# Spectra kept in DRAM as real and imaginary rows side by side, stored and loaded by one transfer per four frequencies

## The chip, the cores and the metric

The kernel runs on one core of a Trainium2 chip. The metric is the device time of one execution in microseconds (us). The kernel before took 2328.96 us (median of 3 runs, 2328.45 to 2333.43).

## What is computed

One layer of an encoder block on 2048 positions of 1024 channels, all in float32. The input is normalised and projected; one quarter of the projection goes through a two-dimensional Fourier transform, the rest through a Hyena operator; both are normalised and projected back, and an MLP follows.

```python
h   = RMSNorm(x)
p   = h @ W_in            # [Fourier group | Hyena x1 | x2 | v], 512 columns each
y_f = RMSNorm_f(Re(FFT2 over positions and group channels))
y_h = RMSNorm_h(Hyena: z = v; for n, gate in (x1, x2): z = gate * long_conv(z, k[n]))
x   = x + concat(y_f, y_h) @ W_out
x   = x + relu(RMSNorm(x) @ W_fc1)^2 @ W_fc2
out = RMSNorm_final(x)

def fft_long_conv(u, k_freq, d):        # the long convolution, twice per channel
    uf = rfft(u, n=2 * l)
    y = irfft(uf * k_freq, n=2 * l)[:, :l]
    return y + u * d
```

The change touches `k_freq`, the spectra of the long filters: 512 channels, two orders, 2048 frequencies, complex.

## The kernel before, in words

The work goes in stages on TensorE (PE): the projections (`project`), the Fourier group (`fourier`), the filters and their spectra (`filters`), the two long convolutions (`hyena`), then the output projection and the two MLP layers, which take most of the time. Transforms are matrix products in two steps, 64 x 64, with a transpose by VectorE (DVE) between.

**The filters.** A `Unit` is 128 channels (`ct`, 0 to 3) of one order (`n`, 0 or 1), eight units in all. `generate` makes the filter in eight pieces; every second piece loads 512 KB of a decay table (`dec`, two buffers). `stage1` is the first transform step (`mm3`, then a transpose into `Gk`), `stage2` the second: for each `q` of 0 to 7 four products of 128 x 128 into one PSUM bank (`pk2`, L572), one per frequency slot. On the 128 partitions of that bank stand 64 real rows and then 64 imaginary rows; the free axis is 4 slots x 128 channels. ScalarE (ACT) copies the bank to the SBUF tile `ks` (L575). Two `q` share one tile of 8 slots (three buffers), and after the second SyncE (SP) issues a store of 512 KB to the DRAM tensor `spec` of that unit (L577): 128 rows of 4 KB. That is 4 stores per unit, 32 in all. Stages of one unit and generation of the unit after next are interleaved by hand (`GENERATE`).

**The convolutions.** A `Block` is 128 channels of one order, eight blocks. `first` and `second` are the two transform steps of the signal. For each `q`, `spectrum` (L647) loads the spectrum of four slots into a tile `ks` of [128, 2, 4, 128] (four buffers), in which each half of the partitions holds both the real (index 0) and the imaginary part (index 1): the complex product needs the real part beside both halves of `pz2`, and the imaginary part beside both halves of the turned copy `zs`. In DRAM the real rows are the first 64 of `spec` and the imaginary rows the last 64, so L650 views them as 64 partitions x 2 parts x 2 KB, and L651 and L652 send this to the lower and then to the upper half of the partitions: two transfers of 256 KB per `q`, 16 per block, 128 in all. At `q` = 0 two small operations (L655, L657) set the slot of the zero frequency right. Then ACT makes `zs` (L676, L677), DVE multiplies by the real part (L679), GpSimd (POOL) by the imaginary part (L680), one of them adds (L681), and `inverse` (L689) needs the sum `y`. `load` (L645) brings the gate of a block, `xg`, 1 MB in rows of 512 B. The loop at L714 interleaves three blocks: the second step of one, the inverse of the one before, the first step of the next, whose first spectrum is loaded at `q` = 7.

All these transfers are issued by SP, which takes them in program order and waits at each until its buffer is free or its source is written. A scheduler orders each engine's instructions from the order of the code and its own estimates.

Of the kernel before, what the change touches and what calls it, by code (L numbers as in the profile page):

```python
# [10 lines left out]
F32 = mybir.dt.float32  # L11
# [116 lines left out]
P = 128  # L128
# [6 lines left out]
def hybrid_block(ctx: ExitStack, tc: tile.TileContext, A, out):  # L135
    nc = tc.nc
# [4 lines left out]
    def scratch(name, shape):  # L141
        return dram.tile(shape, F32, tag=name, name=name)

    gd = [scratch(f"gates{i}", [P, NT, 512]) for i in range(3)]
    kd = [[scratch(f"spec{i}{n}", [P, 32, 128]) for n in range(2)] for i in range(4)]
    wfd = scratch("wfd", [1024, 512])
    embd = scratch("embd", [P, 32, P])
    xtd = [scratch(f"xt{t}", [P, 8, P]) for t in range(NT)]
# [13 lines left out]
    def pool(name, side="left"):  # L162
        return tc.tile_pool(name=name, bufs=1, side=side, reuse_waits="tile")

    def pa(nm):
        return ps.tile([P, 512], F32, tag="a", name=nm, bufs=8)
# [304 lines left out]
    def filters(ctx, fp, gp, zp, zzs, norms, emb, wo, e1k, f2):  # L471
# [9 lines left out]
        p = pa("plongd")  # L481
# [3 lines left out]
        class Unit:  # L485
# [83 lines left out]
            def stage2(self, q):  # L569
                p = pa("pk2")  # L570
                for j in range(4):
                    nc.tensor.matmul(p[:, 128 * j : 128 * j + 128], lhsT=f2[:, 4 * q + j, :], rhs=self.G[:, :, 4 * q + j], start=True, stop=True)  # L572
                if q % 2 == 0:
                    self.ks = sp.tile([P, 8, 128], F32, tag="ks", name="ks", bufs=3)
                nc.scalar.copy(self.ks[:, 4 * (q % 2) : 4 * (q % 2) + 4, :], p.rearrange("p (f c) -> p f c", f=4))  # L575
                if q % 2:
                    nc.sync.dma_start(kd[self.ct][self.n][:, 4 * q - 4 : 4 * q + 4, :], self.ks)  # L577

        units = [Unit(ct, n) for n in range(2) for ct in range(4)]
        for u in units[:2]:  # L580
# [7 lines left out]
        sp = ctx.enter_context(pool("spectra", "right"))  # L588
# [41 lines left out]
    def hyena(hp, wp, rp, zz, e1, b1, f2, a2, out_weights, out_ahead):  # L630
# [6 lines left out]
        class Block:  # L637
# [9 lines left out]
            def spectrum(self, q):  # L647

                ks = hp.tile([P, 2, 4, 128], F32, tag="ks", name="ks", bufs=4)
                src = kd[self.ct][self.n][:, 4 * q : 4 * q + 4, :].rearrange("(s p) f c -> p s f c", s=2)  # L650
                for hf in (slice(0, 64), slice(64, 128)):  # L651
                    nc.sync.dma_start(ks[hf], src)  # L652
                if q == 0:

                    nc.scalar.copy(ks[64:65, 0, 0, :], ks[64:65, 1, 0, :])  # L655
                    for h in (0, 64):
                        nc.gpsimd.memset(ks[h : h + 1, 1, 0, :], 0.0)  # L657
                return ks
# [742 lines left out]
```

## Time and profile before

| what | value |
|---|---|
| median of 3 runs | 2328.96 us |
| the profiled execution, its own time | 2339.88 us |
| its span, first to last instruction | 2336.8 us |
| busy: PE, weight loads, DVE, ACT, POOL | 96%, 80%, 65%, 47%, 36% |
| mean granted TensorE clock | 0.986 |
| moved by DMA, mean rate | 468.42 MB, 200 GB/s |
| stores of spectra issued | 484.7 to 637.5 us |
| loads of spectra issued | 638.0 to 840.2 us |

The table is from one profiled execution. The span is divided by the views into stretches with the busy time of each engine, the share of time for which the core's 16 DMA engines were busy on average, and the rate at which they moved bytes. A wait names who waited and for whom, with total, count and longest. "Us to landing" is the time from the issue of a transfer to its completion.

### The profile page before, as it was taken

To read this page: it belongs to the slowest core of one execution; us is meant where nothing else is said; L and a number is where in the kernel's file an instruction comes from. 1 tells how busy PE (TensorE), PEld (TensorE's weight loads), DVE (VectorE), ACT (ScalarE), POOL (GpSimd) and SP (SyncE) were. 2 spreads that over 40 slices of the span, in tenths; PEclk is the share of its full clock that TensorE was granted. 3 is DMA by queue.
4 is the path that set the end of the run, shared out by engine and by line. 5 is a ranking of instruction groups with operands and counts; after the bars stand their busy time and mean duration, and the time that the engine had idled before them with its cause. 6 is when DMAs were issued, how large, how long until landed. Compare 5 with 4: busy or idle time off the path is not lost. (4 is left out here: it accounts for less than half of the span.)

```text
span 2336.8 us, 31028 instructions
## 1 busy us (share of the span) xinstructions
PE 2250.9 (96%) x11025; PEld 1860.4 (80%) x11025; DVE 1514.5 (65%) x2248; ACT 1106.6 (47%) x1826; POOL 840.6 (36%) x633
## 2 busy tenths in 40 slices
PE   7999998999899979998999999999999999999998
PEld 6887787799787858886788877888888888888886
DVE  6998666677577774547544457444466666866667
ACT  6554211466455554544555556555543333533334
POOL 3345322567465522215755556555400000000000
PEclk9999999999999989999999999999999999999999
DMA  7535888457688986567544456444479666866631
GB/s 250 181 137 176 290 308 321 144 199 233 214 201 188 200 218 189 177 182 237 161 150 152 152 204 208 152 150 149 149 279 373 234 191 198 284 207 193 198 117 72
DMA packets 294780, 468.42 MB, mean 200 GB/s; under 512 B 18453, under 2 KB 142687, under 8 KB 290273
## 3 DMA queue, kind: packets, MB, share of 16 engines
q1 hardware_dynamic: 291265, 460.43, 61.9%
q10 hardware_dynamic: 3360, 6.02, 0.8%
q8 instruction: 86, 1.41, 0.3%
q14 instruction: 69, 0.57, 0.1%
HBM read 312.54 MB, written 152.27 MB: 199 GB/s over the span
## 5 line engine op out<-in xcount | busy, mean ns | idle before, releaser
L181 ACT CAST qahm<-ra 128x1024 fp32r<-128x1024 f32 x110 | 116.0, 1054 | 345.8 <-PE p2u L190 172.0
L182 DVE TENSOR_TENSOR qalm<-ra,qahm 128x1024 fp32r<-128x1024 f32 x110 | 134.7, 1224 | 154.8 <-ACT qahm L181 151.7
L1183 POOL TENSOR_TENSOR acc<-acc,gfin 128x512 f32<-128x512 f32 x4 | 5.1, 1278 | 632.9 <-DMA out<-acc 625.4
L189 PE MATMUL pu<-wh,xh 128*128 128x512 f32 x512 | 206.4, 404 | 5.8 <-ACT wh L184 4.8
L190 PE MATMUL pu<-wl,xh 128*128 128x512 f32 x512 | 203.3, 397 | 5.9 <-DVE wl L182 3.7
L191 PE MATMUL pu<-wh,xl 128*128 128x512 f32 x512 | 203.2, 397 | 5.7 <-DVE xl L182 5.7
L190 PE MATMUL p2u<-qblm,qahm 128*128 128x512 f32 x504 | 196.2, 389 | 0.3 <-DVE qblm L182 0.3
L189 PE MATMUL p2u<-qbhm,qahm 128*128 128x512 f32 x504 | 195.9, 389 | 0.0
L191 PE MATMUL p2u<-qbhm,qalm 128*128 128x512 f32 x504 | 195.8, 389 | 0.0
L397 POOL TENSOR_TENSOR acc<-acc,cw 128x512 f32<-128x512 f32 x45 | 60.9, 1353 | 206.1 <-DVE acc L374 204.8
L182 DVE TENSOR_TENSOR qblm<-rb,qbhm 128x1024 fp32r<-128x1024 f32 x110 | 134.0, 1219 | 1.1 <-ACT qbhm L181 1.1
L181 ACT CAST ahm<-s 128x512 fp32r<-128x512 f32 x124 | 76.7, 621 | 94.0 <-PE p1v L190 54.1
L190 PEld LDWEIGHTS pu<-wl,xh 128*128 128x128 f32 x512 | 98.3, 192 | 28.7 <-DVE wl L182 4.1
L191 PEld LDWEIGHTS pu<-wh,xl 128*128 128x128 f32 x512 | 98.2, 192 | 28.3 <-DVE xl L182 7.7
L189 PEld LDWEIGHTS pu<-wh,xh 128*128 128x128 f32 x512 | 98.0, 192 | 27.8 <-ACT wh L184 6.2
L182 POOL TENSOR_TENSOR alm<-W,ahm 128x512 fp32r<-128x512 f32 x63 | 85.5, 1358 | 91.4 <-ACT ahm L181 91.4
L181 ACT CAST qbhm<-rb 128x1024 fp32r<-128x1024 f32 x110 | 115.3, 1048 | 4.6 <-DMA a1m<-c 2.8
L190 PEld LDWEIGHTS p2u<-qblm,qahm 128*128 128x128 f32 x504 | 94.6, 188 | 20.3 <-DVE qblm L182 0.8
L189 PEld LDWEIGHTS p2u<-qbhm,qahm 128*128 128x128 f32 x504 | 94.6, 188 | 20.2 <-issue 0.3
L191 PEld LDWEIGHTS p2u<-qbhm,qalm 128*128 128x128 f32 x504 | 94.6, 188 | 19.6
L181 ACT CAST ahm<-W 128x512 fp32r<-128x512 f32 x94 | 57.6, 615 | 103.4 <-PE p1u L190 100.8
L191 PE MATMUL p1u<-bm,alm 128*128 128x512 f32 x252 | 99.9, 396 | 6.4 <-DVE alm L182 6.4
(387 smaller groups left out, 6456.8 us busy)
## 6 DMA issues: line engine op xcount, KB each, us to landing
W<-in_w_fc SPq DMA_DIRECT2D x66, 512.0 KB, 4.6
ks<-spec SPq DMA_DIRECT2D x128, 256.0 KB, 6.8
rb<-td SPq DMA_DIRECT2D x64, 512.0 KB, 4.1
ra<-a1m SPq DMA_DIRECT2D x56, 512.0 KB, 6.0
ra<-a0m SPq DMA_DIRECT2D x54, 512.0 KB, 10.7
rb<-in_w_fc SPq DMA_DIRECT2D x46, 512.0 KB, 4.5
f<-in_w_fc SPq DMA_DIRECT2D x16, 1024.0 KB
td<-f SPq DMA_DIRECT2D x16, 1024.0 KB, 4.7
```

The lines of the kernel that those rows point to most:

```text
L181: nc.scalar.copy(hi, src)
L182: (eng or nc.vector).tensor_sub(lo, src, hi)
L189: nc.tensor.matmul(o, lhsT=lh, rhs=rh, start=start, stop=False, skip_group_check=more)
L190: nc.tensor.matmul(o, lhsT=lh, rhs=rl, start=False, stop=False, skip_group_check=more)
L191: nc.tensor.matmul(o, lhsT=ll, rhs=rh, start=False, stop=stop, skip_group_check=more)
L397: nc.gpsimd.tensor_add(m1, m1, cw[:, 3, :])
L1183: nc.gpsimd.tensor_mul(acc[i][:, c], acc[i][:, c], gfin[:, c])
```

## The change: what it does, and the diff

The DRAM tensor of a unit's spectrum has the shape [64, 8, 2, 512] in place of [128, 32, 128]: for each of 64 rows, for each `q`, the 512 real numbers and then the 512 imaginary ones, 4 KB in one piece.

The store is made for every `q`: 256 KB from a tile of [128, 512], of which six buffers stand in the room of the three larger ones. Its DRAM side is viewed as 2 parts x 64 rows x 2 KB, with a step of 2 KB between the parts and of 32 KB between rows. There are 64 stores in place of 32.

The load is one transfer per `q`: 64 rows of 4 KB, read twice by a leading dimension of 2 with a step of 0, to 128 partitions of 4 KB. There are 64 loads of 512 KB in place of 128 of 256 KB. The bytes that arrive are the same.

```diff
-    kd = [[scratch(f"spec{i}{n}", [P, 32, 128]) for n in range(2)] for i in range(4)]
+
+    kd = [[scratch(f"spec{i}{n}", [64, 8, 2, 512]) for n in range(2)] for i in range(4)]
...
-                if q % 2 == 0:
-                    self.ks = sp.tile([P, 8, 128], F32, tag="ks", name="ks", bufs=3)
-                nc.scalar.copy(self.ks[:, 4 * (q % 2) : 4 * (q % 2) + 4, :], p.rearrange("p (f c) -> p f c", f=4))
-                if q % 2:
-                    nc.sync.dma_start(kd[self.ct][self.n][:, 4 * q - 4 : 4 * q + 4, :], self.ks)
+                ks = sp.tile([P, 512], F32, tag="ks", name="ks", bufs=6)
+                nc.scalar.copy(ks, p)
+                nc.sync.dma_start(kd[self.ct][self.n].rearrange("p q s x -> s p q x")[:, :, q], ks)
...
                 ks = hp.tile([P, 2, 4, 128], F32, tag="ks", name="ks", bufs=4)
-                src = kd[self.ct][self.n][:, 4 * q : 4 * q + 4, :].rearrange("(s p) f c -> p s f c", s=2)
-                for hf in (slice(0, 64), slice(64, 128)):
-                    nc.sync.dma_start(ks[hf], src)
+                src = kd[self.ct][self.n][:, q].rearrange("p s x -> p (s x)")
+                nc.sync.dma_start(ks.rearrange("p s f c -> p (s f c)"), src.unsqueeze(0).broadcast_to([2, 64, 1024]))
```

PE's instructions stand in the same order as before. On SP the order around the two kinds of transfer changes. At the start of the filters' stores, SP's instructions before (a row gives the line, what is written and read, and the counts of the written side, outermost first; `spec_60`, `spec_62` and so on are the tensors of the units, `dec` a table's piece):

```order
L577 DMA spec_60<-ks 128x1024 x2
L170 DMA dec<-in_decay 128x1024
L577 DMA spec_60<-ks 128x1024 x2
L170 DMA dec<-in_decay 128x1024 x3
L577 DMA spec_62<-ks 128x1024 x2
```

Each store has 128 as its outermost count. The same place with the change:

```order
L576 DMA spec_60<-ks 2x64x512 x4
L171 DMA dec<-in_decay 128x1024
L576 DMA spec_60<-ks 2x64x512 x4
L171 DMA dec<-in_decay 128x1024 x3
L576 DMA spec_62<-ks 2x64x512 x4
```

Twice as many stores stand between the same loads, and the outermost count of what a store writes is 2. At the start of the convolutions, SP before (`ks` is the tile of a spectrum, `xg` the gate's):

```order
L652 DMA ks<-spec_60 64x2x512 x14
L652 DMA ks<-spec_62 64x2x512 x2
L652 DMA ks<-spec_60 64x2x512 x2
L652 DMA ks<-spec_62 64x2x512 x6
L645 DMA xg<-gates_58 128x16x128
L652 DMA ks<-spec_62 64x2x512 x6
```

Loads of a spectrum come in pairs, one for each half of the partitions. With the change (`yf` is a tile of the Fourier group's result, needed by the output projection):

```order
L650 DMA ks<-spec_60 128x1x1024 x4
L644 DMA xg<-gates_58 128x16x128
L650 DMA ks<-spec_60 128x1x1024
L644 DMA xg<-gates_58 128x16x128
L650 DMA ks<-spec_60 128x1x1024 x2
L650 DMA ks<-spec_62 128x1x1024
L650 DMA ks<-spec_60 128x1x1024
L774 DMA yf<-yfd 64x2x256
L650 DMA ks<-spec_62 128x1x1024
```

The row shows the written side alone, whose outermost count is 128; the read side's is the 2 of the repeated reading. The loads of the gate and those of the first `yf` tiles have moved ahead, the latter from behind the last spectrum to the first blocks.

## The prediction, as put on record before the run

> **What bounds the kernel now.** I read the page first, then the stretches of the two stages that the change touches, then the transfers in them.
>
> ```profile
> span 2336.8 us, 31028 instructions
> ...
> PE 2250.9 (96%) x11025; PEld 1860.4 (80%) x11025; DVE 1514.5 (65%) x2248; ACT 1106.6 (47%) x1826; POOL 840.6 (36%) x633
> ...
> DMA packets 294780, 468.42 MB, mean 200 GB/s; under 512 B 18453, under 2 KB 142687, under 8 KB 290273
> ```
>
> PE is busy for 96% of the span: it is the bound of the whole, and a transfer matters only where it starves PE. When the spectra are stored and loaded stands in the view of the tensor `spec` (duration of an issue, then first and last start):
>
> ```profile
> L652 SPq DMA_DIRECT2D ks<-spec x128: 573/605/4610, 638.0 to 840.2; - x128
> L577 SPq DMA_DIRECT2D spec<-ks x32: 319/320/1562, 484.7 to 637.5; - x32
> ...
> DMA to landing us min/median/max: 2.9/6.0/9.6
> ```
>
> So the filters' stores fill 484.7 to 638, and the convolutions' loads 638 to 840. Those two stretches by engine, and a third from the second MLP layer in which the DMA engines were never idle (the last two columns are their mean busy share and rate):
>
> ```profile
> core 0: us, PE busy (x) PEld busy (x) DVE busy (x) ACT busy (x) POOL busy (x), PEclk, DMA share, GB/s
> 484.50:638.00 153.50, 143.93 (x1054) 130.67 (x1053) 104.20 (x182) 85.71 (x172) 100.02 (x83) 0.98 0.64 217
> 638.00:840.00 202.00, 190.22 (x1323) 165.32 (x1321) 152.11 (x236) 110.67 (x192) 116.55 (x104) 0.99 0.88 199
> ...
> 1740.00:1780.00 40.00, 40.00 (x178) 32.93 (x177) 28.81 (x32) 18.06 (x18) 0.00 (x0) 1.00 1.05 390
> ```
>
> PE is busy for 143.9 of 153.5 us and 190.2 of 202 us, so 9.6 and 11.8 us are all that faster transfers could win in the two. The DMA engines are busy for 0.64 and 0.88 of the time: in the second stage they have little to spare, even with all sixteen at work. In that stage this is who waits for a spectrum, or for a product that needs one:
>
> ```profile
> POOL zs L680 <- DMA ks<-spec: 27.4, 16, 6.0
> ...
> PE pv L689 <- DVE y L681: 13.2, 12, 3.8
> ```
>
> POOL waits 27.4 us for spectra, and PE's 13.2 us of waiting for `y` are partly what follows from it.
>
> **On how many engines a transfer runs.** The question is how the new shapes are spread. Their outermost counts are 2 on one side (the DRAM side of the store, the repeated side of the load) and 128 on the other. The trace has transfers whose outermost count is 128 or 64, and a few with 63. All of the convolutions' stretch:
>
> ```profile
> GB/s 255 233 152 217 204 193 111 269 232 229 198 129 238 232 138 235 80 118 269 228 224 200 67 266 232 228 232 47 264 213 228 231 83 183 238 234 229 159 168 258
> DMA packets 32197, 40.13 MB, mean 199 GB/s; under 512 B 2075, under 2 KB 16411, under 8 KB 32180
> ...
> ks<-spec SPq DMA_DIRECT2D x127, 256.0 KB, 6.8
> xg<-gates SPq DMA_DIRECT2D x7, 1024.0 KB, 12.7
> ```
>
> No row of these transfers is under 512 B, and yet there are 2075 such packets for 134 transfers: 15.5 each, that is 16 but for the edges of the stretch. I read them as one closing packet from each engine that took part. The queue of ACT, which at 25 to 60 us carries only the neighbours' rows of the projection, tests that reading:
>
> ```profile
> GB/s 407 407 426 398 335 225 183 169 19 148 155 229 386 243 120 211 346 302 311 150 112 183 224 256 151 188 55 0 0 0 37 66 206 435 410 337 7 5 152 215
> ...
> q10 hardware_dynamic: 608, 1.04, 11.1%
> ...
> nb<-full ACTq DMA_DIRECT2D x4, 128.0 KB, 2.3
> nb<-full ACTq DMA_DIRECT2D x4, 126.0 KB
> ```
>
> Four transfers of 64 rows of 2 KB (L384, L387) and four of 63 (L385, L388) leave 608 packets. With 16 closing packets for each of the first, 4 x (64 + 16) = 320 are theirs, and 288 are left for the others: 72 each, 63 rows and 9 closing packets. Nine is the largest number up to 16 that divides 63. So a count that sixteen does not divide costs engines, and for an outermost count of 2 the same reading gives two engines. The Trainium skill says this outright (DMA: Bandwidth & Descriptors, Rules for kernel authors, the row on using all 16 engines): a leading zero-stride broadcast of c copies confines the whole transfer to at most c engines. The trace agrees for 63 rows; no transfer of it has a repeated outermost dimension, so for that case the page stands alone.
>
> **The price of one engine.** When all sixteen are busy (1740 to 1780 us) they move 390 GB/s: 24.4 GB/s each. The highest slice above, 435, gives 27.2; the filters' stretch gives 217 / (16 x 0.64) = 21.2. I take 24.4, the row in which nothing but the engines bounds, and keep 27.2 and 21.2 as the ends. The convolutions' own 199 / (16 x 0.88) = 14.1 comes from small rows and from sixteen engines that write to half the partitions at once, and is left out.
>
> **The stores, part by part.** A store moves 256 KB, 131,072 B on each of two engines: 5.37 us at 24.4 GB/s (4.82 to 6.18). 64 of them are 344 us. The other transfers of that stretch:
>
> ```profile
> spec<-ks SPq DMA_DIRECT2D x32, 512.0 KB, 3.7
> dec<-in_decay SPq DMA_DIRECT2D x20, 512.0 KB, 4.0
> zz<-gates SPq DMA_DIRECT2D x4, 1024.0 KB
> a<-in_a SPq DMA_DIRECT2D x1, 2048.0 KB
> ```
>
> Each engine was busy 0.64 x 153.5 = 98 us there, of which the old stores took 32 x 32,768 B / 24.4 GB/s = 43, so 55 us stay for the rest. The two engines need 344 + 55 = 399 us for what PE gives out in 153.5: they become the bound of the stage, which grows by 245 us. Behind a late store wait, in turn, its buffer (one of six), ACT's copy, PE's next bank. The decay loads run on all engines, and so wait on these two behind up to six stores; where a load then comes late, the two run dry for some us. Twelve such places with up to 4 us each bound that at 0 to 50 us; I take nothing, as two `dec` buffers let SP ask ahead.
>
> The 64 issues on SP cost nothing: at some 0.6 us each (L652's row) they are 38 us in 399. ACT's copies are the same 64.
>
> **The loads.** A load moves 512 KB into SBUF, 262,144 B on each of two engines: 10.74 us (9.64 to 12.36). 64 of them are 688 us. The eight gate loads come on top. In the rates above, each `xg` shows as about one slice of 5 us with a low rate (111, 80, 67, 47, 83), so 8 x 5 = 40 us (30 to 50). Together 728 us; before it was 638.0 to the landing of the last load, 840.2 + 6.8 = 847, or 209 us. The stage grows by 519 us. With four buffers and a `q` that takes PE some 3 us (202 us by 64), the next load is always queued, so the two engines never idle. SP's issues fall from 128 to 64, which is worth nothing, since SP would not be waited for. The `yf` loads that moved ahead are off the path: after 847 the old order had them on it, but I see at most a few us there and count none.
>
> The skill also has a price for one engine, about 27 GiB/s (same page, Specifications). By it a load would take 9.0 us and the time would come to about 2930 us; the measured rate stands against it.
>
> **The sum.** 2339.88 + 245 + 519 = 3104 us for a profiled execution. That of before lies 11 us above the median of the runs, so **3093 us**. With 27.2 GB/s and the small ends (308 + 50 and 617 + 30) it is about 2970; with 21.2 GB/s and some dry time (396 + 55 + 40 and 791 + 50) about 3300.
>
> **The rivals.**
>
> *It does what it is written to do, on sixteen engines.* Then the rows of a load double to 4 KB and the writes go to all partitions at once; the wait for spectra goes and PE's idle 11.8 us of the second stage shrink. The skill's rule on two transfers to disjoint partition halves (same table: they share the engines, use one 128-partition transfer) would have it so. The time would be 2317 at best; half of the idle time is other waits, so 2323. What speaks for it: the SBUF side does count 128, and a generator could split by that. What speaks against: 63 rows got nine engines and were not split otherwise. It decides by the number of engines: 33.55 MB at 24.4 GB/s are 1375 engine-us, and 202 - 40 us are free for them, so from nine engines on the stage stays PE's, and below it the loads set its length. Chance 0.06, most of it faster.
>
> *The transfer is made as two halves after all,* each of 64 rows on sixteen engines, as before: 2329, no change. Chance 0.02.
>
> *Only one kind is confined.* If the store is split by its SBUF side, 2329 + 519 = 2848; if only the store is confined, 2329 + 245 = 2574. Both sides of both kinds carry a 2 and a 128, so I see no reason for a difference: 0.02.
>
> *Two engines are enough,* because alone they run faster. To hide the loads each would have to move 16.8 MB in 162 us, 104 GB/s, four times the best slice: no chance of its own.
>
> **How the numbers follow.** The confined case has 0.90, and nine tenths of it lie in 2970 to 3300; the range is that, 0.81 in all. A change of 0.2% (5 us, the spread of the three runs) is what can be told from none. Faster 0.05, same 0.03, slower 0.92.
>
> **What would show it.** If two engines carry each new transfer, packets under 512 B fall from 18453 by 160 x 16 and rise by 128 x 2, to about 16,150; with sixteen they would be about 17,940. The DMA share of the convolutions falls to about 0.2, the rate to under 60 GB/s, the waits for `ks<-spec` grow to hundreds of us, and a load lands some 40 us after its issue, four deep in the queue. PE's busy time stays near 2250 us. A stage of the convolutions near 200 us with a DMA share under 0.88 would prove the step on the engines wrong; loads spaced by much more or less than 10.7 us would prove the price wrong.

## The result, and the profile after

The changed kernel took 3045.41 us (median of 4 runs, 3040.69 to 3050.72), the kernel before in the same sessions 2330.1 us: a ratio of 1.3068, with a 95% interval of 1.3036 to 1.3099. 3093 us were forecast, in a range of 2970 to 3300. The profiled execution of the changed kernel took 3045.94 us, with a span of 3044.2 us: 707.4 us more than the span before.

The page of the changed kernel, its busy line and the rows of its slices (each 76 us):

```profile
span 3044.2 us, 31007 instructions
...
PE 2372.4 (78%) x11025; PEld 1950.8 (64%) x11025; DVE 1514.4 (50%) x2248; ACT 1105.7 (36%) x1826; POOL 839.5 (28%) x633
...
PE   8998996555533333444349989999999999999998
...
PEclk9999998877666766767669999999999999999999
DMA  7447953233121111111145565446444497676651
GB/s 238 167 157 281 338 190 116 79 102 110 76 66 63 53 63 62 63 62 64 57 143 173 177 225 165 149 145 223 162 150 150 167 386 233 193 238 232 194 186 56
DMA packets 288380, 468.41 MB, mean 154 GB/s; under 512 B 16149, under 2 KB 140383, under 8 KB 283873
```

The same two rows before (each slice 58 us):

```profile
PE   7999998999899979998999999999999999999998
...
DMA  7535888457688986567544456444479666866631
```

The hole is in plain sight: between the 7th and the 21st slice PE is busy for about half of the time and then for a third, and the DMA engines fall with it, in the longer second part to a tenth or two of their time and to some 60 GB/s. PE starves there, and little moves. Before the 7th and behind the 21st slice PE is busy for most of the time, as it was throughout in the kernel before. The bytes are the same but for 0.01 MB (468.41 MB), and the packets under 512 B are 16149, where the text on record had "about 16,150" for two engines per new transfer.

The tensor `spec` in the changed kernel (issue time min/median/max, first and last start; then who waited for it, total us and times):

```profile
L576 SPq DMA_DIRECT2D spec<-ks x64: 485/4788/11188, 478.2 to 849.4; - x64
L650 SPq DMA_DIRECT2D ks<-spec x64: 482/5427/21207, 854.5 to 1534.5; - x64
...
  ACT ks L653: 371.3, 8
  DVE y L677: 322.0, 45
  POOL ks L655: 312.4, 8
  POOL zs L678: 308.0, 39
  ACT ks L575: 77.8, 18
```

ACT, DVE and POOL, which touch a loaded spectrum, now wait for it, for over 300 us each, and the copies of the filters wait for their stores (78 us). The stretches of the two stages and of what follows (the columns are those of the table by engine: busy time, then granted clock, DMA share and GB/s):

```profile
478.20:854.50 376.30, 203.00 (x1142) 173.57 (x1140) 104.92 (x191) 86.56 (x174) 100.55 (x84) 0.76 0.26 89
854.50:1560.50 706.00, 265.76 (x1284) 222.11 (x1284) 156.36 (x243) 117.09 (x205) 120.00 (x107) 0.65 0.19 63
1560.50:3044.00 1483.50, 1450.28 (x6440) 1186.64 (x6440) 882.36 (x1234) 709.16 (x1118) 423.15 (x294) 0.99 0.58 190
```

The filters take 376 us from the first store to the first load (153 before). From there to 1560.5 us, where the last wait for a spectrum ends, it is 706 us (209 before). What follows takes 1483.5 us, against 1490 from 847 us on before.

How wide a single transfer is can be read off a stretch of 20 us in which nothing but loads of spectra moves:

```profile
1000.00:1020.00 20.00, 5.82 (x31) 5.36 (x32) 6.62 (x12) 7.96 (x15) 6.27 (x5) 0.57 0.13 52
```

A share of 0.13 of sixteen engines is two engines, and 52 GB/s are 26 GB/s for each. The packets fit: before, the trace has 18070 packets of 4 B, now 15766. The 2304 fewer are 160 x 16 - 128 x 2, which is one such closing packet for each engine of a transfer.

### The profile page after: what moved, and what is told of

Its sections match the earlier page's. It is cut to its first block, busy times and chain, and to the rows that moved or that the text cites. A ratio compares the mean times of both kernels' runs of the same rounds, so it can differ in the third digit from the quotient of the medians.

```text
span 3044.2 us, 31007 instructions
## 1 busy us (share of the span) xinstructions
PE 2372.4 (78%) x11025; PEld 1950.8 (64%) x11025; DVE 1514.4 (50%) x2248; ACT 1105.7 (36%) x1826; POOL 839.5 (28%) x633
## 2 busy tenths in 40 slices
DMA packets 288380, 468.41 MB, mean 154 GB/s; under 512 B 16149, under 2 KB 140383, under 8 KB 283873
## 5 line engine op out<-in xcount | busy, mean ns | idle before, releaser
L687 PE MATMUL pv<-y,a 128*128 128x128 f32 x512 | 105.2, 371 | 305.1 <-ACT V L688 133.2
L687 PEld LDWEIGHTS pv<-y,a 128*128 128x128 f32 x512 | 92.5, 271 | 318.6 <-ACT V L688 134.6
L677 DVE TENSOR_TENSOR y<-pz,ks 128x512 f32<-128x512 f32 x64 | 43.8, 685 | 377.5 <-DMA ks<-spec 322.0
L671 PE MATMUL pz<-G,f 128*128 128x128 f32 x512 | 95.1, 342 | 107.4 <-DVE G L419 48.8
L678 POOL TENSOR_TENSOR zs<-zs,ks 128x512 f32<-128x512 f32 x64 | 82.7, 1297 | 347.0 <-DMA ks<-spec 308.0
L671 PEld LDWEIGHTS pz<-G,f 128*128 128x128 f32 x512 | 89.9, 254 | 118.7 <-DVE G L419 51.6
L664 PE MATMUL pz<-zz,e1z 128*128 128x256 f32 x256 | 91.8, 506 | 52.7 <-ACT V L688 25.5
L573 PE MATMUL pk<-Gk,f 128*128 128x128 f32 x512 | 76.7, 309 | 64.2 <-DVE Gk L419 59.7
L509 DVE TENSOR_TENSOR kt<-pk,dec 128x512 f32<-128x512 f32 x64 | 43.0, 678 | 153.7 <-DMA dec<-in_decay 146.0
```

The lines of the kernel that those rows point to most:

```text
L509: nc.vector.tensor_mul(k4, p.rearrange("p (l c) -> p l c", l=4), dec)
L664: nc.tensor.matmul(p[:, 256 * sp : 256 * sp + 256], lhsT=e1[:, sp, :], rhs=zz[:, :, lo : lo + 16], start=True, stop=True)
L677: nc.vector.tensor_mul(y, p3, ks[:, 0])
L678: nc.gpsimd.tensor_mul(zs, zs, ks[:, 1])
L687: nc.tensor.matmul(p[:, 128 * j : 128 * j + 128], lhsT=a2[:, 4 * q + j, :], rhs=self.y[q][:, j, :], start=True, stop=True)
```

## The experiments

Theory **T1**: an outermost count of 2 puts a transfer on two DMA engines, and that alone makes the time. Rivals: **T2**, the new layout is slow (row pitch, smaller stores, more of them); **T3**, reading a row twice by a step of 0 is slow; **T4**, any order of rows but one plain run is slow. All edits are made to the changed kernel unless it is said otherwise.

**Neither transfer with a count of 2.**

```diff
-                nc.sync.dma_start(kd[self.ct][self.n].rearrange("p q s x -> s p q x")[:, :, q], ks)
+                for s, hf in enumerate((slice(0, 64), slice(64, 128))):
+                    nc.sync.dma_start(kd[self.ct][self.n][:, q, s], ks[hf])
...
-                nc.sync.dma_start(ks.rearrange("p s f c -> p (s f c)"), src.unsqueeze(0).broadcast_to([2, 64, 1024]))
+                for hf in (slice(0, 64), slice(64, 128)):
+                    nc.sync.dma_start(ks[hf].rearrange("p s f c -> p (s f c)"), src)
```

> The new layout in DRAM is kept; each store is made as two of 64 rows (real, then imaginary), each load as two of 64 rows of 4 KB, one for each half of the partitions. No transfer has an outermost count of 2. Theory T1 (an outermost count of 2 puts a transfer on two DMA engines, and nothing else is slow): back to the time of before, 2310 to 2340 us. Rival T2 (the layout itself is slow: a row pitch of 32 KB, 256 KB stores, six small buffers, more transfers on SP): most of the 715 us stay, over 2800 us.

Measured: 2355.98 us, 1.0088 of before (1.0059 to 1.0118). With the same layout 689 of the 715 us are gone: T2 falls. But it is not the time of before; 21 us are left, outside what T1 expected. They lie in the filters. The stretch from the first store to the first load, and PE's waits in it:

```profile
483.40:666.50 183.10, 159.71 (x1084) 144.05 (x1083) 108.18 (x188) 86.87 (x173) 100.83 (x84) 0.91 0.72 186
```

```profile
PE pdk L545 <- DVE dk L534: 10.8, 4, 3.8
PE psum_k L529 <- POOL acc L523: 8.6, 2, 7.4
```

PE's longest wait there before (it had none for `dk`):

```profile
PE psum_k L528 <- POOL acc L522: 6.2, 1, 6.2
```

The stage takes 183 us where it took 153. PE waits 10.8 us for `dk`, a small product in the normalising of a filter, for which it did not wait before, and its granted clock, the share of its full clock that it is given, is 0.91 in place of 0.98. The loads' stage is 197 us long, 5 less than before. The last runs below come back to the filters.

**One term at a time.** The stores as in the change with the loads in halves, and the reverse.

> Stores as in the change (outermost count 2), loads as two halves of 64 rows. T1: the store's term alone. In the trace of the change the stretch from the first store to the first load is 376 us where it was 153, so 2330 + 223 = 2553 us (2530 to 2590). If stores cost nothing by themselves (only the loads are confined): 2330 us.

> Stores as two halves of 64 rows, loads as in the change (one transfer, a leading count of 2 with step 0). T1: the load's term alone, 680 us from the first load to the last where it was 202: 2330 + 478 = 2808 us (2780 to 2860). If the two terms add up, this and the run with confined stores together make 2330 + 715. T2: no smaller than the change's 3045 us, since the layout is the same.

Measured: 2560.5 and 2841.57 us, one run each, beside 2334.95 for before. The transfers of `spec`, for the confined stores and for the confined loads:

```profile
L651 SPq DMA_DIRECT2D ks<-spec x128: 444/594/4694, 856.6 to 1062.1; - x128
L576 SPq DMA_DIRECT2D spec<-ks x64: 478/4798/11001, 480.3 to 851.4; - x64
```

```profile
L577 SPq DMA_DIRECT2D spec<-ks x128: 445/580/1757, 476.5 to 658.1; - x128
L651 SPq DMA_DIRECT2D ks<-spec x64: 474/5852/21253, 659.5 to 1328.3; - x64
```

Both times lie within what was expected. Each stage is long only where its own transfer has the count of 2: 376 us for the stores, 669 us for the loads. Each page counts 18069 packets under 512 B, which is what two engines for the one kind and sixteen for the other give (18453 - 32 x 16 + 64 x 2 for the stores). The extra times are 226 and 507 us; the second kernel has the half stores, which with half loads cost 21 us, so 226 + 486 = 712 against the change's 715. The terms add up.

**The repetition kept, the count changed.**

```diff
-                nc.sync.dma_start(ks.rearrange("p s f c -> p (s f c)"), src.unsqueeze(0).broadcast_to([2, 64, 1024]))
+                nc.sync.dma_start(ks.rearrange("p s f c -> p (s f c)"), src.unsqueeze(1).broadcast_to([64, 2, 1024]))
```

> Stores as two halves; one load of 512 KB per q that reads each row twice, as in the change, but with the 64 rows as the outermost count and the repetition inside it. The rows then land two by two on neighbouring partitions, so the spectra meet the wrong numbers: only the time counts. T1: 64 is spread over sixteen engines, 2310 to 2335 us, and this is what the change would have given had its transfer been spread. Rival T3 (reading a row twice by a step of 0 is what is slow, whatever its place): 2800 us and more.

Measured: 2339.84 us, 1.0022 of before (1.0010 to 1.0033), 5 us above the top of what T1 expected. The row is still read twice by a step of 0, in one transfer of 512 KB, and 500 us of the load's term are gone: T3 falls. Filters and loads by stretch:

```profile
483.70:667.20 183.50, 159.86 (x1084) 144.34 (x1083) 108.26 (x188) 86.91 (x173) 100.90 (x84) 0.91 0.72 185
667.20:852.80 185.60, 181.30 (x1282) 158.48 (x1281) 144.19 (x235) 111.47 (x195) 116.23 (x104) 0.99 0.74 225
```

The convolutions take 186 us from the first load to the last, 17 less than before, and move 225 GB/s at a DMA share of 0.74 where it was 199 at 0.88. So the merging of two halves does help when it is spread over all engines. The half stores, which this kernel needs too, take it back: the filters are at 183 us again. An engine moved 225 / (16 x 0.74) = 19.0 GB/s while busy, and 199 / (16 x 0.88) = 14.1 with the halves of before, so with the halves each of the sixteen engines was also slower. The length of a row has little to do with it: the kernel with halves has the same rows of 4 KB and moved 203 GB/s at 0.86 in its loads, 14.8 for each engine. The Trainium skill (DMA: Bandwidth & Descriptors, Rules for kernel authors) would have one transfer over all partitions in place of two over halves, since both share the same engines. The trace agrees with the advice, and shows that the shared engines are not the whole reason.

**The count without the repetition: 2, 4 and 8.** Two loads of 64 rows for each `q`, with the rows in k interleaved runs; stores in halves. The edit for a count of 2 (4 and 8 in place of the last number otherwise):

```diff
-                nc.sync.dma_start(ks.rearrange("p s f c -> p (s f c)"), src.unsqueeze(0).broadcast_to([2, 64, 1024]))
+                for hf in (slice(0, 64), slice(64, 128)):
+                    nc.sync.dma_start(ks[hf].rearrange("p s f c -> p (s f c)"), src.rearrange("(a b) x -> b a x", b=2))
```

> As the run with all transfers in halves (2356 us), but each load of 64 rows takes them in another order: row 0, 2, 4 ... and then 1, 3, 5 ..., so that its outermost count is 2 (2 x 32 rows of 4 KB). No row is read twice. The spectra meet the wrong frequencies; only the time counts. T1: two engines again, 128 loads x 131,072 B / 26 GB/s = 645 us and 40 for the gates in place of 197: 2356 + 488 = 2844 us, as with the repeated read (2842); packets under 512 B 18453 - 160 x 16 + 128 x 16 + 128 x 2 = 18197. T3 (the repetition is what is slow): 2356 us.

> The same with the rows taken in four interleaved runs, outermost count 4. T1: four engines, 128 x 65,536 B / 26 GB/s = 323 + 40 = 363 us in place of 197: 2356 + 166 = 2522 us (2490 to 2550); packets under 512 B 18453. Rival T4 (any order other than one run over all rows falls back to a slow path, whatever the count): about 2840 us.

> The same with eight interleaved runs, outermost count 8. T1: eight engines, 161 + 40 = 201 us of transfers against the 197 that the stage takes without them as a bound: 2356 to 2385 us; packets under 512 B 18965. This is the point from which the number of engines decides, put at nine in the prediction with the lower rate. T4: about 2840 us.

Measured: 2837.4, 2524.6 and 2396.42 us, one run each, beside 2335.26 for before. The rates from 700 to 850 us, in the middle of the loads, for counts of 2, 4 and 8 in this order (each number is a slice of 3.75 us):

```profile
GB/s 52 51 51 52 52 52 51 56 52 52 51 51 52 52 52 51 51 52 210 112 47 55 52 42 46 52 52 52 50 52 52 52 51 51 52 52 52 50 57 52
```

```profile
GB/s 107 104 105 105 150 207 101 104 82 99 104 102 105 105 105 102 116 223 127 105 86 94 105 105 105 104 106 93 102 178 187 102 96 67 97 103 108 105 104 104
```

```profile
GB/s 202 167 201 202 209 208 91 173 220 150 152 153 172 196 201 210 226 181 208 206 201 144 82 185 211 192 208 209 206 125 156 226 152 167 196 211 208 114 167 212
```

The plateaus are 52, 104 and 208 GB/s: 26 GB/s for each unit of the count. The packets under 512 B over the whole program were 18197, 18453 and 18965, each the expected number to the last packet. T3 and T4 fall, and T1 holds at five numbers of engines: 2, 4 and 8 by rate and packets, 9 (the 63 rows) and 16 by packets. Eight engines kept 26 GB/s each while they wrote to half the partitions; the 14.8 above are for sixteen at once. The count of 8 came out at 2396 us, above the 2385 expected: its loads fill 232 us, not 201. By the sums the transfers and PE's work are nearly equal there, and POOL's products wait 73 us for `ks` in that stage; that each side holds up the other now and then is how we read it, and no run separates it.

**Can the gain be kept?** Three kernels in which all that is stored and loaded is spread. In the first the spectrum stands twice in DRAM, on 128 rows, and one load of 128 rows brings it.

```diff
-    kd = [[scratch(f"spec{i}{n}", [64, 8, 2, 512]) for n in range(2)] for i in range(4)]
+    kd = [[scratch(f"spec{i}{n}", [P, 8, 2, 512]) for n in range(2)] for i in range(4)]
...
+                if q % 2 == 1:
+                    for d, queue in ((slice(0, 64), nc.sync), (slice(64, 128), nc.scalar)):
+                        for s, hf in enumerate((slice(0, 64), slice(64, 128))):
+                            queue.dma_start(kd[self.ct][self.n][d, q - 1 : q + 1, s], self.ks[hf])
...
-                nc.sync.dma_start(ks.rearrange("p s f c -> p (s f c)"), src.unsqueeze(0).broadcast_to([2, 64, 1024]))
+                nc.sync.dma_start(ks.rearrange("p s f c -> p (s f c)"), src)
```

> A version meant to be right and spread: the spectrum stands twice in DRAM, 128 rows of 32 KB, so that one load of 128 rows of 4 KB fills both halves of the partitions on sixteen engines. For each pair of q there are four stores of 64 rows (real and imaginary part, to each copy), two of them issued by ACT. T1: the convolutions take 186 us where before took 202, as in the run with the repetition inside (16 us won); the stores move twice the bytes, 33.5 MB, some 43 us more of DMA time in a stage with 55 free. 2315 us if the filters stay at 153 us, 2345 if they take 183 as with the half stores. If transfers on two engines were not the cause, it would stay above 2800.

Measured: 2342.99 us, 1.0043 of before (1.0026 to 1.0059): 16 us won in the loads (661.7 to 848.3 us), 26 lost in the filters (482.7 to 661.7). The higher of the two expectations.

The second asks whether the filters lose by the number of stores or by the order of the engines' work. It is the kernel with halves, with stores for two `q` at once:

```diff
...
+                if q % 2:
+                    for s, hf in enumerate((slice(0, 64), slice(64, 128))):
+                        nc.sync.dma_start(kd[self.ct][self.n][:, q - 1 : q + 1, s], self.ks[hf])
...
```

> As the run with all transfers in halves (2356 us), but stores wait for two q: 64 stores of 64 rows of 2 x 2 KB in place of 128. ACT, DVE and PE stand in nearly the order of that run (32 rows of difference, where that run has 127 to before). Theory S (the 30 us that the filters lost there come from the order in which the scheduler put ACT's and DVE's work): they stay, 2345 to 2360 us. Rival N (they come from the number of stores that SP issues): half of them or more go, 2325 to 2340 us.

Measured: 2349.58 us, 1.0066 (1.0042 to 1.0090). Its transfers and PE's longest wait in the filters:

```profile
L654 SPq DMA_DIRECT2D ks<-spec x128: 444/594/4222, 656.6 to 854.0; - x128
L579 SPq DMA_DIRECT2D spec<-ks x64: 574/598/1372, 480.7 to 654.4; - x64
```

```profile
PE pdk L545 <- DVE dk L534: 10.4, 4, 2.9
```

With half as many stores the filters still take 176 us, and PE still waits 10.4 us for `dk`. So most of the 30 us are not in the number of stores. Nor does anything wait long for the transfers themselves: ACT's copies wait 0.8 us for a store here, and in the kernel with halves DVE waits 0.9 us for the decay loads. What the traces do show is another order on DVE, from `vk` (the sum of squares of a filter) to `dk`. The fourth filter before:

```profile
524.22 0.16 DVE L530 TENSOR_SCALAR vk<-psum_k 128x1 f32<-128x1 f32 x1
525.28 0.69 DVE L508 TENSOR_TENSOR kt<-pk,dec 128x512 f32<-128x512 f32 x1 [0.90 <-PE pk L504]
...
528.66 0.26 DVE L533 TENSOR_SCALAR dk<-vk,nw_k,longd 128x1 f32<-128x1 f32 x1
```

The same filter in the kernel with halves:

```profile
528.09 0.16 DVE L531 TENSOR_SCALAR vk<-psum_k 128x1 f32<-128x1 f32 x1
528.78 0.69 DVE L509 TENSOR_TENSOR kt<-pk,dec 128x512 f32<-128x512 f32 x1 [0.53 <-POOL k L183]
...
530.73 0.69 DVE L509 TENSOR_TENSOR kt<-pk,dec 128x512 f32<-128x512 f32 x1 [0.20 <-ACT sqr L519]
533.29 0.69 DVE L509 TENSOR_TENSOR kt<-pk,dec 128x512 f32<-128x512 f32 x1 [1.87 <-ACT k L182]
...
535.69 0.27 DVE L534 TENSOR_SCALAR dk<-vk,nw_k,longd 128x1 f32<-128x1 f32 x1
```

PE's instructions stand in the same order in both. On DVE three products with the decay table (`kt`) now stand between `vk` and `dk` where one stood, the last of them waits for ACT, and `dk` comes 7.6 us after `vk` in place of 4.4. In the kernel with the change's own stores and half loads one product stands there, and `dk` comes 4.2 us after `vk`, although those stores are slow:

```profile
580.00 0.15 DVE L531 TENSOR_SCALAR vk<-psum_k 128x1 f32<-128x1 f32 x1
580.28 0.69 DVE L509 TENSOR_TENSOR kt<-pk,dec 128x512 f32<-128x512 f32 x1
...
584.18 0.26 DVE L534 TENSOR_SCALAR dk<-vk,nw_k,longd 128x1 f32<-128x1 f32 x1
```

So the loss goes with the order that the scheduler sets for the half stores. How much of it this order makes is not shown: no run changed the order alone.

The third keeps the stores of before and makes the second tensor by copies inside DRAM, issued by SP or by ACT.

```diff
...
+                if q == 7:
+                    for d in (slice(0, 64), slice(64, 128)):
+                        for s, hf in enumerate((slice(0, 64), slice(64, 128))):
+                            src = kd[self.ct][self.n][hf].rearrange("p (q f) c -> p q (f c)", q=8)
+                            nc.sync.dma_start(kd2[self.ct][self.n][d, :, s], src)
...
```

> The stores of before are kept (32 of 128 rows); after each unit's last store four transfers inside DRAM, 1 MB each and issued by SP, make a second tensor in which the spectrum stands twice, in the layout of the run with two copies; the loads are the 64 spread ones of that run (186 us for the convolutions, 16 less than before). 33.5 MB more are moved, 86 us of DMA time at 390 GB/s, where the filters have 55 us free and the convolutions some 50: 2315 us if it all fits, 2345 and more if the decay loads wait behind the copies or the order of ACT and DVE costs as much as before.

> The same with the copies issued by ACT, in its order, and so waited for there: each copy waits for the unit's last store to land (3.7 us), eight times. 2315 us if nothing else moves; 2345 if these waits hold up ACT's casts.

Measured: 2400.6 us, 1.0289 (1.0263 to 1.0315), and 2386.2 us, 1.0232 (1.0195 to 1.0268): the first at the bad end of what was expected, the second beyond it. With SP's copies the first load starts at 715.7 us where it was 638. Three of the waits in its filters:

```profile
PE psum_k L529 <- POOL acc L523: 42.2, 5, 15.1
...
ACT ks L576 <- PE pk L573: 34.5, 32, 4.7
...
ACT ks L576 <- DMA spec<-ks: 26.7, 5, 13.3
```

ACT's copies out of PSUM now wait for stores, and the normalising (`psum_k`) comes late as well; that the copies in DRAM hold up the stores is how we read it. No kernel of this study is faster than the one before.

## Why the prediction was right, point by point

**The engines.** The step that carried the prediction, two engines for an outermost count of 2, was read from 63 rows that left nine closing packets. It held, for the DRAM side of a store as for the repeated side of a load. The Trainium skill's rule on a leading zero-stride broadcast (DMA: Bandwidth & Descriptors, Rules for kernel authors), for which no transfer before could speak, agrees with the 16149 packets and with the share of 0.13.

**The price of one engine** was the term that was mis-sized. 24.4 GB/s was taken from a stretch with all sixteen busy; two alone ran at 26. (The 14.1 that was left out was put down to small rows and to half the partitions; at 14.8 with rows of 4 KB the runs leave mainly the second.) At 26 a store takes 5.04 us and a load 10.08, 968 us for all, 64 less than forecast. The 27 GiB/s for one engine in the Trainium skill (the same page, Specifications), 29 GB/s, which the prediction set aside, are above what was measured; the time lies between the 2930 us estimated from them and the forecast.

**The sum.** The two engines were to be busy for 399 + 728 = 1127 us from the first store on. From 478.2 to 1560.5 us it was 1082: 64 less by the price, and 19 more that no view splits among the gate loads, the other transfers of the filters and gaps. Each stage alone compares less well, since the filters' last stores were still in the queue when the first loads were issued. The first store also came 6.5 us earlier, as it no longer waits for a second `q`, and the end took 6 us less, with two `yf` tiles loaded ahead (that these are the reason is not shown). 764 - 45 - 6.5 - 6 = 707 us, the measured growth of the span. The 11 us by which the profiled execution of before lay above its median did not recur, so that 3093 came nearer to the 3045 than the 3104 of the working did: those 11 us are luck.

**SP's issues.** "At some 0.6 us each" was wrong: an issue of a store took 4.8 us in the median and one of a load 5.4. SP's rows in the filters of the changed kernel (start, duration, what):

```profile
478.25 10.81 SPq L576 DMA_DIRECT2D spec<-ks  x4
489.17 4.91 SPq L171 DMA_DIRECT2D dec<-in_decay  x1
494.18 16.25 SPq L576 DMA_DIRECT2D spec<-ks  x4
```

After a few transfers SP is held at the pace of the two engines, 4 to 5 us for each store, and the decay loads behind it are held too: DVE waited 146 us for them. It cost little beyond the sum, because the engines stayed fed meanwhile: in neither stage does a slice of the rates (9.4 and 17 us) fall below 46 GB/s. The dry time put at 0 to 50 us is within the 19.

**PE's busy time** was to stay near 2250 us and is 2372. The work is the same (11025 records in the same order); the clock is not (below).

**The rivals.** On sixteen engines the change was to give 2317 to 2323 us. The convolutions did win 17 us in the kernel with the repetition inside, more than the 11.8 of PE's idle time that were given as the bound, in part because work moved behind the stretch (1282 of PE's records in place of 1323). That kernel took 2340 us, since its half stores took more than the gain back in the filters. But half stores are not the change's own. No run has the change's store on sixteen engines, and with it, confined, DVE kept nearly the order of before. Without the loss in the filters an estimate from these rows is 2335 - 17 = 2318 us, so the price of this rival stays open. The rival of two halves was priced at 2329 us, no change, and its kernel took 2356: that half stores could cost anything was missed. For one kind alone 2574 and 2848 us were given, and 2560.5 and 2841.57 were measured.

**The signs.** Packets and waits came as forecast, and the rate, 63 GB/s in the convolutions, a little above the 60. The 40 us from issue to landing stay unread, since the views give no landing time for these transfers.

## What to carry to other kernels

Look at the outermost count of both sides of a transfer before its size: here a repeated read with a leading 2, and a store that puts two halves side by side in DRAM, ran on two engines of sixteen, and 256 KB each at 26 GB/s are 10 us. In these traces, where no row of the transfers is under 512 B, the number of packets under 512 B divided by the number of transfers shows it: 2, 4 or 8 for the confined ones, 16 for the others. And another form of store in a stage where a scheduler sets the order need not be free, even where nothing waits for the stores: here stores of 64 rows, on sixteen engines all, went with 23 to 30 us more in a stage of 153.

## What the runs showed of the hardware that was not expected

An issue on SP can take as long as a transfer ahead of it: 0.3 to 0.6 us in the median with sixteen engines, about 5 with two, and 9.5 us for each of eight loads in a row from 1089 us on, where the price of 26 GB/s gives 10.

The granted clock of PE was lower where PE starved. In the two stages PE was busy for 54% and 38% of the time, and the clock was 0.76 and 0.65; behind them, at 98%, it was 0.99. This is a stretch of the changed kernel in which PE did nothing:

```profile
860.00:880.00 20.00, 0.00 (x0) 0.00 (x0) 0.15 (x1) 1.68 (x4) 0.49 (x3) 0.50 0.13 52
```

The same product took 288 ns in the mean before and 371 ns in the changed kernel (busy time in us, then the mean in ns):

```profile
L689 PE MATMUL pv<-y,a 128*128 128x128 f32 x512 | 73.0, 288 | 16.1 <-DVE y L681 16.0
```

```profile
L687 PE MATMUL pv<-y,a 128*128 128x128 f32 x512 | 105.2, 371 | 305.1 <-ACT V L688 133.2
```

Here this cost little, since PE was waiting anyhow; but PE's busy time rose by 121 us without any work added, so that a busy time alone would have told a false story.
